# A hybrid decoder step on one Trainium2 core: the last block of gate2 rows is made with the other conditioning blocks, and the first expert weights are looked up later

## The chip, the cores and the metric

One core of one Trainium2 chip runs the whole program. The metric is device microseconds of one execution, the median of repeated runs. TensorE (PE) multiplies, VectorE (DVE), ScalarE (ACT) and GpSimd (POOL) do the elementwise work, and SyncE (SP) issues the weight loads. The five engines run their own instruction streams in order and meet at semaphores.

## The reference, cut to what matters

576 tokens (512 of a prompt, 64 of eight samples) go through one layer. Nine conditioning vectors (one for the prompt, one for each sample) give six rows each, of which `gate2` scales the result of the expert layer at the very end.

```python
ada = jax.nn.silu(c) @ prm['w_ada'][l] + prm['b_ada'][l]
sh1, sc1, g1, sh2, sc2, g2 = jnp.split(ada, 6, axis=-1)
xm = x * (1.0 + sc1[:, None, :]) + sh1[:, None, :]
proj = xm @ prm['w_in'][l]
...
merged = (gates[..., 0, :] * (ya @ prm['w_br_a'][l]) + gates[..., 1, :] * (yb @ prm['w_br_b'][l])
          + gates[..., 2, :] * (yc @ prm['w_br_c'][l]) + gates[..., 3, :] * (yd @ prm['w_br_d'][l]))
mix = merged @ prm['w_o'][l]
x = _layer_norm(DN_ALPHA * x + g1[:, None, :] * mix, prm['ln1_g'][l], prm['ln1_b'][l])
xm2 = x * (1.0 + sc2[:, None, :]) + sh2[:, None, :]
f = _hier_moe(xm2, prm['router_g'][l], prm['router_e'][l], prm['w_e_gate'][l], prm['w_e_up'][l],
              prm['w_e_down'][l])
x = _layer_norm(DN_ALPHA * x + g2[:, None, :] * f, prm['ln2_g'][l], prm['ln2_b'][l])
```

The expert layer picks two of 32 SwiGLU experts for each token; each expert has gate and up matrices of 1024x512 and a down matrix of 512x1024.

## The kernel before, in words

**Stages.** In order of time: shift1 and scale1 (until about 33 us); the branches' projections, their own work and their gated products with `w_br`, branch by branch in the order C, B, A, D (until about 761 us); the product with `w_o`, the first LayerNorm and the router's logits for five token tiles in the order `ORD = (0, 1, 4, 2, 3)` (until about 843 us); the router's decisions (`route`), the first two places (`start_moe`); the experts, two at a time, as 16 pairs (`moe`, about 859 to 1352 us); a loop for tokens that found no place (`overflow`, empty here), and the second LayerNorm (`final`).

**Weights.** Every weight tile of 512 KB is loaded on SP's queue by `Pipe.fill` (L242) in the order of one list, `plan`. For each tile `where` names the buffers it takes. In the projections these are four of the tag `raw`; loaded tiles are split into a high and a low part by ACT (L316) and DVE or POOL (L322), unless they are of the kinds `wa`, `w1`, `w2` or belong to the experts. Expert tiles rotate over 26 buffers: 8 of `raw` and `rb`, 10 of `m8`, 8 of `hi` and `lo`. Expert loads keep the program's order among themselves on SP; tile 27 waits until the two tiles of the first matmul pair are read.

**The conditioning blocks.** Shift2, scale2, gate1 and gate2 are eight blocks of 512 columns, each made of four tiles of `w_ada`. Blocks 0 to `NL` - 1 are made during branch A's gates (`gates("A", ...)`, d = 0 to 7): `ada_block` (L577) multiplies two of the four tiles before the branch product of d and `ada_late` two behind it, as four 32-row matmuls side by side in the array, then ACT and DVE add the four parts (L643 to L647) and POOL adds the rows to the DRAM tile `adad` (L648). With `NL` = 7, block 7 (the second half of gate2) is left: its four tiles, called `w2`, stand in the plan behind the first `GA` = 4 expert tiles, and `ada_gate2` (L663) multiplies them as 9-row matmuls that are put behind the last transposes and router logits of the last two token tiles. The last `m` of the eight is read by ACT (L665) and added to `adad` by POOL (L666). The buffers of the four `w2` tiles then serve the last four of the first 26 expert tiles.

**The router and the first places.** Router logits (L1508, L1510) of the last token tile end the LayerNorm stage. `route` (DVE, L1554 to L1573) makes the choice `Mb`, small matmuls (L1578, L1579) count places, `place` finds the tokens of a pair of experts (L1640, L1651), and `fetch` (L1667 to L1670) gathers their rows by an indirect DMA on POOL. Behind the second of the index casts (L1668) DVE has in its stream: the residual rows (L1516, L1517), then, mixed, the routing weights (`weights`, to `Whl`, L1603 and L1604) and the table of blocks (`blocks`, to `nbi`, L1631).

**The first pair of experts.** `gate_up` multiplies eight gate tiles, then eight up tiles (L1746), in four steps of two tiles each (c = 0 to 3); behind c = 1 and c = 3 it calls `some(n, m)`, which issues n combine pieces and m `parts`. All of these matmuls keep the program's order on PE. Before, one part is issued in each of the four slots of pair 0: `weigh(0)` (L1651, needs `Whl`) behind c = 1 of the gate, `columns(1)` (transposes of the second pair's rows, L1683) behind c = 3, `weigh(1)` and `place(2)` in the up half. The routing weight that `weigh(0)` makes is first read when the down product of pair 0 is scaled (L1714).

**One register load.** `overflow` reads the number of blocks into a register of every engine (`nb = nc.values_load(s.nbi[0:1, 0:1], ...)`, L1855). On SP this load stands among the expert tiles' loads, at a place that is fixed when the program is built.

Of the kernel before, what the change touches and what calls it, by code (L numbers as in the profile page):

```python
# [20 lines left out]
F32 = mybir.dt.float32  # L21
# [169 lines left out]
BME = lambda nc: nc.vector  # L191
HP0 = 2000
N0 = 8
GA = 4
NL = 7
GM = (1, 1, 1, 1, 1)
ND = 6
NW = 3
BP = 1
# [3 lines left out]
class Pipe:  # L203


    def __init__(s, k, plan, hi_pool, nh, where, bufs):
        s.k, s.plan, s.hip, s.nh, s.where, s.bufs = k, plan, hi_pool, nh, where, bufs
        s.nl = s.ns = s.ng = 0
        s.raw, s.hl, s.held, s.dma, s.rel, s.hook = {}, {}, {}, {}, [], {}

        s.m8free, s.m8n, s.m8cur = 0, 0, None

        s.raws = set(i for i, c in enumerate(plan) if c[0] in ("w1", "w2", "wa") or i >= k.moe0)

    def fill(s):
        nc = s.k.nc
# [61 lines left out]
        return ws[0][0] if n == 1 else [w[0] for w in ws]  # L278

    def get(s, nm):  # L280
        while s.plan[s.ng][0] in ("w1", "w2", "wa"):
            s.ng += 1
        i = s.ng
        assert s.plan[i][0] == nm, (s.plan[i][0], nm)
        s.ng += 1
        s.fill()
        s.split()
        s.fill()
        return s.hl.pop(i)

    def pair(s, nm):

        while s.plan[s.ng][0] == "w2":
            s.ng += 1
        i = s.ng
        assert s.plan[i][0] == s.plan[i + 1][0] == nm, (s.plan[i][0], nm)
        s.ng += 2
        s.fill()
        ws = [s.raw.pop(j) for j in (i, i + 1)]
        for _, tag, rc in ws:  # L300
            if rc is not None:
                rc[0] -= 1
            if rc is None or rc[0] == 0:
                s.rel.append(tag)
        return [w[0] for w in ws]


class K:
# [198 lines left out]
    def plan_front(s):  # L507
        A = s.A
        pl = []
        for i in range(16):  # L510
            pl.append(("w1", A["wa1"][i], 1024))
        for i in range(12):
            pl.append(("ct", A["wct"][i], 1024))

        def gates(k, w, kt):
            pl.append(("gl", A["wgl"][k * 8], 1024))
            for d in range(8):
                if d < 7:
                    pl.append(("gl", A["wgl"][k * 8 + d + 1], 1024))
                late = k == 0 and d < NL  # L520
                if late:
                    for h in range(AB):
                        pl.append(("wa", A["wa"][d, h], 1024))
                pl.append(("br", w[d], kt * 128))
                if late:
                    for h in range(AB, 4):
                        pl.append(("wa", A["wa"][d, h], 1024))
        gates(2, A["wbr"][16:24], 4)
        for i in range(12, 16):
            pl.append(("ct", A["wct"][i], 1024))  # L530
        for i in range(4):
            pl.append(("wv", A["wv"][i], 1048))
        gates(1, A["wbr"][8:16], 4)
        for i in range(16, 30):
            pl.append(("ct", A["wct"][i], 1024))
        gates(0, A["wbr"], 4)
        for i in range(30, 36):
            pl.append(("ct", A["wct"][i], 1024))
        gates(3, A["wbd"], 6)

        s.wo0 = len(pl)
        for _ in range(2):
            for k in range(8):
                pl.append(("wo", A["wo"][k], 1024))
        s.moe0 = len(pl)
        s.mi = {}

        def add(nm, ap):
            if len(s.mi) == GA:
                s.wag = len(pl)  # L550
                for i in range(NL * 4, 32):
                    pl.append(("w2", A["wa"][i // 4, i % 4], 1024))
            s.mi[len(pl)] = len(s.mi)
            pl.append((nm, ap, 1024))

        def pair(e, c0, c1):
            for c in range(c0, c1):
                for i in range(2):
                    add(("wg", "wu", "wd")[c // 4], A["we"][e + i, c])
        pair(0, 0, 8)  # L560
        for e in range(0, 32, 2):
            if e < 30:
                pair(e + 2, 0, 8)
            pair(e, 8, 12)
        s.plan = pl
        s.nwa = 0
# [70 lines left out]
    def ada_late(s, b, p):  # L637
# [8 lines left out]
            nc.scalar.copy(r, p[g:g + 9])  # L646
            nc.vector.tensor_tensor(o, o, r, OP.add)  # L647
        nc.gpsimd.dma_start(s.adad[:, b * 512:b * 512 + 512], o, accum_op=OP.add)  # L648

    def ada_gate2(s):  # L650

        nc = s.nc
        a = [s.trs[ORD[4], 0], s.trs[ORD[4], 1], s.lgs[ORD[4]], s.trs[ORD[3], 0], s.trs[ORD[3], 1], s.lgs[ORD[3]]]
        q = [x for x, m in zip(a, GM) for _ in range(m)]
        for b in range(NL, 8):
            p = s.ms()
            for h in range(4):
                w = s.pipe.take(s.wag + 4 * (b - NL) + h)
                for kk in range(2):
                    k = 2 * h + kk  # L660
                    x = q.pop(0) if q else a[-1]
                    with s.tc.issue_after(x.ins), s.tc.high_priority(offset=300):
                        nc.tensor.matmul(p[:9], s.sil[:, k, :9], w[:, kk * 512:(kk + 1) * 512], start=(k == 0), stop=(k == 7))  # L663
            o = s.lp.tile([9, 512], F32, name="g2", tag="xt", bufs=2)
            nc.scalar.copy(o, p[:9])  # L665
            nc.gpsimd.dma_start(s.adad[:, b * 512:b * 512 + 512], o, accum_op=OP.add)  # L666

    def cond_rows(s):

# [603 lines left out]
    def build2(s):  # L1273
# [72 lines left out]
        for i in range(base, len(s.plan)):  # L1346
            m = s.mi.get(i, -1)
            if m < 0 or len(seq) < GA:
                t = (s.ring, "raw") if n9 % (NR + NB) < NR else (s.raw2, "rb")
                n9 += 1  # L1350
                if seq and m < 0:
                    late.append(t)
            elif len(seq) < GA + len(late):
                t = late[len(seq) - GA]
            else:
                t = seq[-(GA + len(late))]
            tags[i] = t
            if m >= 0:
                seq.append(t)
# [54 lines left out]
        rp = s.g2p  # L1414
        s.LG = rp.tile([128, 5, 36], F32, name="LG")
        nc.vector.memset(s.LG, 0.0)
        s.trs, s.lgs = {}, {}
        acc = {}

        def wo(t, k, w):  # L1420
# [48 lines left out]
    def ln1(s, t, acc):  # L1469
# [30 lines left out]
        for h in range(2):  # L1500
            p = s.ms() if P is None else P[:, h]
            for k in range(4):
                kk = 4 * h + k
                s.trs[t, h] = nc.tensor.transpose(p[:, k * n:(k + 1) * n], src[:, kk * 128:(kk + 1) * 128], s.cc("ident")[:n, :n])
            nc.scalar.copy(xt[:, 4 * h:4 * h + 4, :n], p[:, :4 * n].rearrange("p (k t) -> p k t", k=4))
        p = s.ms()
        for k in range(8):
            s.lgs[t] = nc.tensor.matmul(p[:n, :36], xt[:, k, :n], rt[:, k, :], start=(k == 0), stop=(k == 7))  # L1508
        if t < 4:
            V.scalar_tensor_tensor(s.LG[:, t, :], p[:, :36], rstd, s.rb, op0=OP.mult, op1=OP.add)  # L1510
        else:
# [252 lines left out]
    def moe(s):  # L1764
# [42 lines left out]
            n = iter(slots)  # L1807
            return s.gate_up(lambda k, o: s.xg[p][:, k, o * 64:o * 64 + 64], lambda c: c % 2 and some(*next(n)))
        s.columns(0)
        parts += [(lambda: s.weigh(0, s.ms()),), (s.columns, 1), (lambda: s.weigh(1, s.ms()),), (s.place, 2)]  # L1810
        h = s.hidden(gu(0, [(0, 1)] * 4), pe=s.pe)
        for p in range(16):
            if 0 < p < 14:
                parts.append((s.place, p + 2))
# [167 lines left out]
def body(tc, A, NB=4):  # L1982
    with ExitStack() as ctx:
# [1 line left out]
        k.NB = NB  # L1985
        k.build()
        k.build2()
        k.ada_gate2()
        k.route(0, 5, k.lp)
        k.start_moe()  # L1990
        k.le.close()
# [28 lines left out]
```

## Time and profile before

| | |
|---|---|
| median of 3 runs | 1388.23 us (1386.42 to 1388.26) |
| the profiled execution | 1388.56 us |
| its span, first to last instruction | 1386.7 us |
| PE busy | 1309.0 us, 94% of the span |
| DVE, ACT, POOL busy | 776.7, 408.8, 320.4 us |
| HBM | 307.16 MB read, 9.78 MB written, 229 GB/s over the span |
| mean granted TensorE clock | 0.953 |

The span is what the first and last instruction bound; 1.9 us of the profiled time lie around it. A matmul record's end is modelled, so PE's busy time says that something was in the engine, not that it worked at its peak; an fp32 matmul leaves two records. Idle time in square brackets is that of the engine just before the row, with what ended it.

### The profile page before, as it was taken

To read this page: it belongs to the slowest core of one execution; us is meant where nothing else is said; L and a number is where in the kernel's file an instruction comes from. 1 tells how busy PE (TensorE), PEld (TensorE's weight loads), DVE (VectorE), ACT (ScalarE), POOL (GpSimd) and SP (SyncE) were. 2 spreads that over 40 slices of the span, in tenths; PEclk is the share of its full clock that TensorE was granted. 3 is DMA by queue.
4 is the path that set the end of the run, shared out by engine and by line. 5 is a ranking of instruction groups with operands and counts; after the bars stand their busy time and mean duration, and the time that the engine had idled before them with its cause. 6 is when DMAs were issued, how large, how long until landed. Compare 5 with 4: busy or idle time off the path is not lost. (4 is left out here: it accounts for less than half of the span.)

```text
span 1386.7 us, 20311 instructions
## 1 busy us (share of the span) xinstructions
PE 1309.0 (94%) x7962; PEld 944.1 (68%) x7962; DVE 776.7 (56%) x1333; ACT 408.8 (29%) x657; POOL 320.4 (23%) x335
## 2 busy tenths in 40 slices
PE   7997899999999999999999987999999999999992
PEld 5997899999999877788899863344334444444331
DVE  3799797572676356667524487244444334434347
ACT  3311222642463424556422332021111111111114
POOL 1796004051321315333333151000000000000003
PEclk6998999999999989899999997999999999999997
DMA  9522123222322354361222969899999999999972
GB/s 378 151 76 61 54 92 110 69 69 84 108 77 84 113 200 170 129 230 43 72 85 93 320 241 358 340 414 414 414 415 414 415 413 415 414 415 415 415 296 99
DMA packets 90376, 318.15 MB, mean 229 GB/s; under 512 B 11113, under 2 KB 11265, under 8 KB 90271
## 3 DMA queue, kind: packets, MB, share of 16 engines
q1 hardware_dynamic: 83176, 293.29, 55.6%
q0 software_dynamic: 6528, 22.63, 4.8%
q8 instruction: 63, 1.03, 0.3%
q10 hardware_dynamic: 576, 0.93, 0.2%
q14 instruction: 33, 0.27, 0.1%
HBM read 307.16 MB, written 9.78 MB: 229 GB/s over the span
## 5 line engine op out<-in xcount | busy, mean ns | idle before, releaser
L1746 PE MATMUL mh<-raw,xg 128*64 128x512 f32 x1024 | 247.7, 605 | 0.2 <-DMA raw<-in_we_dram 0.2
L589 PE MATMUL mm<-xh,wh 128*128 128x288 f32 x1088 | 244.0, 305 | 2.9 <-DVE ebs L708 2.4
L589 PE MATMUL mm<-xh,wl 128*128 128x288 f32 x1088 | 240.4, 302 | 2.1 <-DVE wl L322 2.1
L589 PE MATMUL mm<-xl,wh 128*128 128x288 f32 x1088 | 240.4, 301 | 0.0
L316 ACT CAST wh<-raw 128x1024 fp32r<-128x1024 f32 (+3 forms) x120 | 113.1, 948 | 316.5 <-PE mm L589 228.3
L322 DVE TENSOR_TENSOR wl<-raw,wh 128x1024 fp32r<-128x1024 f32 (+3 forms) x112 | 133.3, 1194 | 130.1 <-ACT wh L316 129.7
L589 PEld LDWEIGHTS mm<-xh,wh 128*128 128x128 f32 x1088 | 180.9, 194 | 5.7 <-issue 3.3
L589 PEld LDWEIGHTS mm<-xh,wl 128*128 128x128 f32 x1088 | 178.8, 192 | 4.8 <-DVE wl L322 3.2
L589 PEld LDWEIGHTS mm<-xl,wh 128*128 128x128 f32 x1088 | 179.2, 193 | 0.4 <-issue 0.3
L1746 PEld LDWEIGHTS mh<-raw,xg 128*64 128x64 f32 x1024 | 75.2, 138 | 132.8 <-issue 117.4
L1793 DVE TENSOR_TENSOR x<-x,mc 128x512 f32<-128x512 f32 x120 | 78.2, 682 | 124.3 <-PE mc L1732 124.3
L1703 PE MATMUL mh<-raw,h 128*64 128x512 f32 x512 | 130.2, 601 | 1.0 <-ACT h L1761 0.7
L1670 POOL DMA_INDIRECT gr<-xmd,idi x16 | 16.2, 1010 | 415.9 <-PE mh L1746 385.4
L720 DVE SCALAR_TENSOR_TENSOR acc<-ebp,prm,acc 128x512 f32<-128x512 f32 x120 | 104.9, 883 | 2.1
L1703 PEld LDWEIGHTS mh<-raw,h 128*64 128x64 f32 x512 | 40.4, 136 | 72.0 <-issue 56.6
L1715 ACT CAST yh<-y 128x512 fp32r<-128x512 f32 x32 | 19.8, 620 | 220.9 <-DVE y L1714 207.4
L632 POOL TENSOR_TENSOR merged<-merged,sg 128x576 f32<-128x576 f32 x23 | 43.2, 1877 | 108.9 <-DVE sg L631 108.8
L1714 DVE SCALAR_TENSOR_TENSOR y<-mh,ws,G 128x512 f32<-128x512 f32 x32 | 24.0, 751 | 70.2 <-PE mh L1703 70.2
L1732 PEld LDWEIGHTS mc<-yh,ohT 128*128 128x128 f32 x120 | 22.4, 187 | 52.1 <-issue 47.1
L1732 PE MATMUL mc<-yh,ohT 128*128 128x512 f32 x120 | 53.6, 447 | 0.0
L1750 ACT ACTIVATE sg<-mh 128x512 f32<-128x512 f32 x16 | 9.6, 597 | 128.5 <-issue 78.6
L1732 PE MATMUL mc<-yl,ohT 128*128 128x512 f32 x120 | 47.4, 395 | 0.0
(436 smaller groups left out, 2010.3 us busy)
## 6 DMA issues: line engine op xcount, KB each, us to landing
raw<-in_we_dram SPq DMA_DIRECT2D x384, 512.0 KB
raw<-in_wa_dram SPq DMA_DIRECT2D x48, 512.0 KB
raw<-in_wct_dram SPq DMA_DIRECT2D x36, 512.0 KB
raw<-in_wgl_dram SPq DMA_DIRECT2D x32, 512.0 KB
raw<-in_wo_dram SPq DMA_DIRECT2D x16, 512.0 KB
raw<-in_wbr_dram SPq DMA_DIRECT2D x24, 256.0 KB
s<-in_st_ssm_dram POOLq DMA_DIRECT2D x4, 768.0 KB, 4.8
out_ssms_dram<-s POOLq DMA_DIRECT2D x4, 768.0 KB, 4.7
```

The costliest lines, as they stand in the source:

```text
L316: r = s.nc.scalar.copy(out, in_)
L322: r = (s.nc.gpsimd if pool else s.nc.vector).tensor_tensor(out, full, hi, OP.subtract)
L589: nc.tensor.matmul(p[:m, hf, :288], w, xk[:, hf * 288:(hf + 1) * 288], start=(k == 0 and n == 0), stop=(k == kt - 1 and n == 2))
L632: (nc.vector if nm == "D" and d == 7 else nc.gpsimd).tensor_tensor(m, m, sg, OP.add)
L720: nc.vector.scalar_tensor_tensor(o, i, wt, o, op0=OP.mult, op1=OP.add)
L1670: s.glast = nc.gpsimd.indirect_dma_start(out=gr[:n], out_offset=None, in_=s.xmd[:, :], in_offset=bass.IndirectOffsetOnAxis(ap=ix[:n, 0:1], ...
L1703: s.dlast = s.pe(nc.tensor.matmul(p[r], h[:, f, r], ws[o][:, kk * 512:(kk + 1) * 512], start=(f == 0), stop=(f == 3), skip_group_check=True))
L1714: V.scalar_tensor_tensor(y, p, ws, s.G2[0][:, hf * 512:hf * 512 + 512], op0=OP.mult, op1=OP.mult)
L1715: nc.scalar.copy(yh, y)
L1732: m = pe(s.nc.tensor.matmul(p[:r], oT[:n, t * 128:t * 128 + r], y[:n, hf], start=(i == 0), stop=(i == 1)))
L1746: s.pe(nc.tensor.matmul(p[o * 64:o * 64 + 64], xg(k, o), ws[o][:, kk * 512:(kk + 1) * 512], start=(k == 0), stop=(k == 7), skip_group_chec ...
L1793: nc.vector.tensor_tensor(o, o, p[:n], OP.add)
```

## The change

The four tiles of conditioning block 7 are loaded and multiplied in branch A's gates at d = 7, as blocks 0 to 6 are (`NL` = 8); `ada_gate2`, its nine-row matmuls, its copy and its addition to `adad` are gone. `GA` is 8: the first eight expert tiles take the eight buffers of `raw` and `rb`, where before four expert tiles and four `w2` tiles took them; the number of buffers of expert tiles stays 26. In the first pair of experts no part is issued behind c = 1 of the gate; `columns(1)` comes behind c = 3 as before, `weigh(0)` behind c = 1 of the up half, and `weigh(1)` and `place(2)` both behind its c = 3.

```diff
-GA = 4
-NL = 7
-GM = (1, 1, 1, 1, 1)
+GA = 8
+NL = 8
...
         def add(nm, ap):
-            if len(s.mi) == GA:
-                s.wag = len(pl)
-                for i in range(NL * 4, 32):
-                    pl.append(("w2", A["wa"][i // 4, i % 4], 1024))
             s.mi[len(pl)] = len(s.mi)
...
-    def ada_gate2(s):
-
-        nc = s.nc
-        a = [s.trs[ORD[4], 0], s.trs[ORD[4], 1], s.lgs[ORD[4]], s.trs[ORD[3], 0], s.trs[ORD[3], 1], s.lgs[ORD[3]]]
-        q = [x for x, m in zip(a, GM) for _ in range(m)]
-        for b in range(NL, 8):
-            p = s.ms()
-            for h in range(4):
-                w = s.pipe.take(s.wag + 4 * (b - NL) + h)
-                for kk in range(2):
-                    k = 2 * h + kk
-                    x = q.pop(0) if q else a[-1]
-                    with s.tc.issue_after(x.ins), s.tc.high_priority(offset=300):
-                        nc.tensor.matmul(p[:9], s.sil[:, k, :9], w[:, kk * 512:(kk + 1) * 512], start=(k == 0), stop=(k == 7))
-            o = s.lp.tile([9, 512], F32, name="g2", tag="xt", bufs=2)
-            nc.scalar.copy(o, p[:9])
-            nc.gpsimd.dma_start(s.adad[:, b * 512:b * 512 + 512], o, accum_op=OP.add)
...
             if m < 0 or len(seq) < GA:
                 t = (s.ring, "raw") if n9 % (NR + NB) < NR else (s.raw2, "rb")
                 n9 += 1
-                if seq and m < 0:
-                    late.append(t)
...
-        parts += [(lambda: s.weigh(0, s.ms()),), (s.columns, 1), (lambda: s.weigh(1, s.ms()),), (s.place, 2)]
-        h = s.hidden(gu(0, [(0, 1)] * 4), pe=s.pe)
+        parts += [(s.columns, 1), (lambda: s.weigh(0, s.ms()),), (lambda: s.weigh(1, s.ms()),), (s.place, 2)]
+        h = s.hidden(gu(0, [(0, 0), (0, 1), (0, 1), (0, 2)]), pe=s.pe)
...
         k.build2()
-        k.ada_gate2()
         k.route(0, 5, k.lp)
```

## Rows read from the trace of the kernel before

**Rows 1.** Page, 40 equal slices of the span: what the DMA engines moved
```profile
GB/s 378 151 76 61 54 92 110 69 69 84 108 77 84 113 200 170 129 230 43 72 85 93 320 241 358 340 414 414 414 415 414 415 413 415 414 415 415 415 296 99
```

**Rows 2.** Stretches: busy us (records) by engine, clock, DMA share, GB/s
```profile
850.00:860.00 10.00, 4.64 (x25) 3.88 (x27) 8.96 (x16) 1.76 (x5) 4.93 (x6) 0.56 0.95 327
860.00:870.00 10.00, 6.19 (x25) 2.34 (x23) 9.82 (x42) 1.44 (x2) 0.00 (x0) 0.84 0.50 177
870.00:880.00 10.00, 10.00 (x49) 3.85 (x47) 1.65 (x4) 1.65 (x3) 0.00 (x0) 0.91 0.79 288
...
900.00:950.00 50.00, 50.00 (x234) 20.07 (x230) 20.80 (x38) 10.06 (x18) 1.90 (x2) 1.00 1.03 415
...
1335.00:1345.00 10.00, 9.32 (x40) 3.85 (x39) 6.18 (x10) 2.90 (x5) 0.00 (x0) 1.00 0.75 302
```

**Rows 3.** Waits of SP, 890 to 1350 us: us in total, times, longest
```profile
SPq L242 <- DMA raw<-in_we_dram: 310.1, 332, 2.2
```

**Rows 4.** Timeline of SP: the expert tiles' issues around the stall
```profile
848.56 0.33 SPq L242 DMA_DIRECT2D raw<-in_we_dram  x1
862.42 0.80 SPq L242 DMA_DIRECT2D raw<-in_we_dram  x2
870.64 0.81 SPq L242 DMA_DIRECT2D raw<-in_we_dram  x2
```

**Rows 5.** Waits of SP 863.5 to 872 us, and the register load L1855 on SP
```profile
SPq L1855 <- DVE ws L1660: 6.7, 1, 6.7
...
L1855 SPq TENSOR_LOAD <-nbi x1: 472/472/472, 869.7 to 869.7; - x1
```

**Rows 6.** Timeline, DVE: second index cast, `Whl`, `nbi`
```profile
852.76 0.15 DVE L1668 CAST idi<-idf 128x1 int32<-128x1 f32 x1
...
867.50 0.38 DVE L1604 TENSOR_TENSOR Whl<-W,Whl 128x128 fp32r<-128x128 f32 x2
...
869.56 0.14 DVE L1631 CAST nbi<-ca 1x1 int32<-1x1 f32 x1
```

**Rows 7.** Timeline, PE, first pair of experts
```profile
857.60 1.94 PE L1683 MATMUL ms<-cst,gr 128*128 128x128 f32 x8 [4.78 <-DMA gr<-xmd,idi]
859.47 4.64 PE L1746 MATMUL mh<-raw,xg 128*64 128x512 f32 x16
867.92 0.83 PE L1651 MATMUL ms<-Whl,oh 128*128 128x6 f32 x5 [3.81 <-DVE Whl L1604]
...
874.79 3.65 PE L1746 MATMUL mh<-raw,xg 128*64 128x512 f32 x16
```

**Rows 8.** Timeline, the end of the router's logits and the choice
```profile
835.37 1.83 PEld L1508 LDWEIGHTS ms<-rg,xt 128*128 128x128 f32 x8
...
838.28 0.58 ACT L1505 COPY xt<-mm 128x512 f32<-128x512 f32 x1 [1.68 <-PE mm L1504]
...
838.45 3.15 PE L663 MATMUL ms<-raw,sil 128*9 128x512 f32 x4
...
841.53 1.75 PE L1508 MATMUL ms<-rg,xt 128*128 128x36 f32 x14
...
843.21 5.32 PE L663 MATMUL ms<-raw,sil 128*9 128x512 f32 x12
...
847.43 0.33 DVE L1573 TENSOR_TENSOR Mb<-m,m 128x160 bf16<-128x160 f32 x1
848.45 0.10 PEld L1579 LDWEIGHTS <-tsb 128*128 128x128 bf16 x1 [0.86 <-issue]
```

**Rows 9.** Timeline, conditioning block 6 in branch A's gates
```profile
594.54 1.07 PE L577 MATMUL ms<-raw,sil 128*32 128x512 f32 x8
...
598.38 1.06 PE L577 MATMUL ms<-raw,sil 128*32 128x512 f32 x8
```

**Rows 10.** Stretches in branch A's gates, columns as in rows 2
```profile
570.00:575.00 5.00, 3.18 (x26) 2.06 (x24) 3.33 (x13) 2.50 (x5) 0.85 (x2) 0.98 0.00 2
575.00:580.00 5.00, 4.90 (x37) 1.98 (x36) 3.28 (x8) 1.15 (x3) 4.13 (x4) 0.68 0.38 136
```

More of the change, by code (lines that the diff above doesn't have):

```diff
@@ L211, in __init__ @@
         s.m8free, s.m8n, s.m8cur = 0, 0, None
-        s.raws = set(i for i, c in enumerate(plan) if c[0] in ("w1", "w2", "wa") or i >= k.moe0)
+        s.raws = set(i for i, c in enumerate(plan) if c[0] in ("w1", "wa") or i >= k.moe0)
     def fill(s):
@@ L280, in get @@
     def get(s, nm):
-        while s.plan[s.ng][0] in ("w1", "w2", "wa"):
+        while s.plan[s.ng][0] in ("w1", "wa"):
             s.ng += 1
@@ L291, in pair @@
     def pair(s, nm):
-        while s.plan[s.ng][0] == "w2":
-            s.ng += 1
         i = s.ng
@@ L1416, in build2 @@
         nc.vector.memset(s.LG, 0.0)
-        s.trs, s.lgs = {}, {}
         acc = {}
@@ L1503, in ln1 @@
                 kk = 4 * h + k
-                s.trs[t, h] = nc.tensor.transpose(p[:, k * n:(k + 1) * n], src[:, kk * 128:(kk + 1) * 128], s.cc("ident")[:n, :n])
+                nc.tensor.transpose(p[:, k * n:(k + 1) * n], src[:, kk * 128:(kk + 1) * 128], s.cc("ident")[:n, :n])
             nc.scalar.copy(xt[:, 4 * h:4 * h + 4, :n], p[:, :4 * n].rearrange("p (k t) -> p k t", k=4))
@@ L1507, in ln1 @@
         for k in range(8):
-            s.lgs[t] = nc.tensor.matmul(p[:n, :36], xt[:, k, :n], rt[:, k, :], start=(k == 0), stop=(k == 7))
+            nc.tensor.matmul(p[:n, :36], xt[:, k, :n], rt[:, k, :], start=(k == 0), stop=(k == 7))
         if t < 4:
```

## The prediction

> **What bounds the kernel now.** I read the slices of the page first. In the first half the DMA engines move mostly 50 to 230 GB/s; from the middle of the expert stage on they move 414 GB/s in slice after slice [rows 1]. The table of stretches says the same: in 900 to 950 us the DMA share is at its highest value, 1.03, at 415 GB/s, and it falls only behind 1335 us [rows 2]. The waits of SP agree: of the time between 890 and 1350 us SP spends 310.1 us, in 332 waits, on earlier expert tiles' own transfers [rows 3], not on a buffer. So the 384 expert tiles (384 x 0.524 MB = 201 MB, 486 us at 414 GB/s) set the length of that stage, and its end moves only with the moment from which the stream flows without a break. One tile costs 0.524 MB / 414 GB/s = 1.27 us. Ahead of it, in the projections, PE is the bound.
>
> The break is the next thing to see. Twenty-six tiles are on their way by 848.56 us, all buffers are taken, and the next issues come at 862.42 (two tiles) and then only at 870.64 us [rows 4]. Between 860 and 870 us DMA is half idle, and 870 to 880 us still moves 288 GB/s [rows 2]. The first part of the pause ends with PE: its first matmul pair starts at 859.47 us [rows 7]. The second doesn't. The first 16 records (c = 0 and c = 1) are over at 859.47 + 4.64 = 864.1 us [rows 7], so the buffers of the next two tiles are free then, six microseconds before they are loaded. The waits of SP name what holds it: the register load L1855, 6.7 us, and the load itself starts at 869.7 us [rows 5], just behind `nbi`, which DVE ends at 869.56 + 0.14 = 869.70 us [rows 6]. SP works in order, so the tile loads behind L1855 wait for a number that the empty overflow loop needs 480 us later. This hidden wait decides what the change can bring.
>
> **The change, part by part.**
>
> *Block 7 in branch A's gates.* A block costs PE two groups of eight records, 1.07 and 1.06 us [rows 9], 2.1 us, where PE is the bound: +2.1 us for all that follows. Its ACT and DVE adds and its four loads run beside PE there, on a DMA system that is half idle; I cost them at nothing. If that cover fails, it is rival three.
>
> *`ada_gate2` and its nine-row matmuls.* Of its 16 records four (3.15 us) stand in front of the last 14 records of the router's logits, which PE does from 841.53 to 843.28 us; their input was copied at 838.28 + 0.58 = 838.86 us [rows 8]. Without the four, the 14 follow from about 838.5 us. The clock is at half there; eight loads of this kind took 1.83 us [rows 8], 0.23 each, so 14 take 3.2 us and end at 841.7 us: 1.6 us earlier (2.7 us if they ran at the 1.75 us they had). The other twelve records hold PE until 848.45 us, while DVE had `Mb` ready at 847.43 + 0.33 = 847.76 us [rows 8]; of these 0.69 us I take 0.5, since a handoff costs something. Against this, PE is then idle between 841.7 and about 846 us and its clock falls to 1.2 GHz before the counting and place matmuls: some 18 small records on the path, each at most 0.23 - 0.125 us (1.75 / 14) slower, 1.9 us at most, nothing at least. The granted clock was down to 0.56 in 850 to 860 us anyway [rows 2], so a part was slow before; I take 0.4. The chain to the index casts gains 1.6 + 0.5 - 0.4 = 1.7 us (bounds 0 and 3.4).
>
> The Trainium skill ("TensorE: Matmul & The Clock Gate", section "HAM oscillation — how this bites in real kernels") says that pauses of PE put its clock back to half and the next burst starts slow; it speaks against taking filler matmuls away. The rows agree that it happens here.
>
> *Four loads less ahead of the experts.* They took 4 x 1.27 = 5.1 us of DMA. All 26 buffers still fill before PE reads the first; the pause only begins earlier. Nothing, as long as the stream pauses anyway. If the pause were gone, it could be worth up to 5.1 us. The gather, for which PE waited 4.78 us [rows 7], meets less traffic; that too lies in the pause.
>
> *`weigh(0)` later.* It takes 3.81 us of idle PE out of the first gate product: PE waited for `Whl` (867.88 us) [rows 6, 7]. In the new order eight gate tiles, `columns(1)` and four up tiles stand in front, 3 x 3.65 us of matmuls and more [rows 7], so `weigh(0)` comes when `Whl` is long there. But PE isn't the bound of the stage. What it does is free buffers sooner: by the time SP is released, ten or more are free instead of four, and the stream starts at full rate. Before, 870 to 880 us lost (415 - 288) x 10 / 415 = 3.1 us of transfer, 0.64 of it ahead of the issue at 870.64; the remaining 2.4 us are the first transfer's way and a shortage of free buffers. No row parts them: a gain between 0 and 2.4 us; I take a third, 0.8.
>
> *The moment of release.* From the second index cast (852.76 us) to `nbi` (869.56 us) DVE is busy (8.96 and 9.82 of 10 us) [rows 2, 6] with work that the change doesn't touch. So `nbi` moves with the casts, 1.7 us earlier, and SP with it.
>
> The sum: + 2.1 - 1.7 - 0.8 = -0.4 us. The profiled execution took 1388.56 us, 0.33 above the median of 1388.23; from the median this gives 1387.8 us. Its own range, by the bounds (chain 0 to 3.4, restart 0 to 2.4, handing 2.1 in front), is 1384.5 to 1390.3 us.
>
> **The rivals.**
>
> *One: the register load falls behind more tiles.* Its place on SP, between tiles 28 and 29, is fixed when the program is built, and the change moves both sides of it: PE no longer stops behind c = 1, and the gather meets less traffic. Each pair of tiles that gets ahead of it flows in the pause and is worth 2 x 1.27 = 2.5 us. One pair: 1385.3 us. Three or more, or none held at all: the stream runs from the first release, 862.42 - 1.7 = 860.7 us; before, it was worth an unbroken start at 870.64 + 0.8 - 2.5 = 868.9 us; 8.2 less 2.1 is 6.1 us, 1382.1 us. For it: c = 1 was over six microseconds before SP was let go, so the order is out of step with the run. Against: nothing in the change touches L1855 or `nbi`.
>
> *Two: it falls ahead of tiles 27 and 28.* Then the change doesn't bring even the earlier restart: 1387.8 + 2.5 = 1390.3 us. Nothing speaks for it but that the order is made anew.
>
> *Three: the front stalls (slower).* In branch A's gates four buffers serve gate, conditioning and branch tiles in one line. At d = 7 there is no further gate product, and branch tile 7 and the next projection's tiles now stand behind four more loads. If PE waits for one, it loses the wait and then the clock: 570 to 575 us has 1.8 us of idle PE, and 575 to 580 us ran at 0.68 [rows 10], 1.6 us more. Such a gap or two on top of the sum gives some 4 us, 1391.8 us. It decides when PE idles over 3 us there. Against: blocks 0 to 6 go through the same line, and state matmuls of branch D can fill.
>
> *Four: the cold clock eats the chain's gain.* With 1.9 instead of 0.4 us and a logits gain at its low end, `nbi` isn't earlier: 1387.8 + 1.7 = 1389.5 us. By the Trainium skill's rule above this would be the time.
>
> **How the numbers follow.** Forecast 0.34; rival one with one pair 0.22, with three or more 0.22; two 0.05; three 0.10; four 0.07. The single likeliest is the forecast, 1387.8 us. The range that leaves 2 in 10 out reaches to the full rival one and to three: 1381.5 to 1391.5 us. A measurement tells 0.2%, 2.8 us, from no change: below 1385.4 lie all of the large rival one, a good half of the small one and the forecast's edge, 0.40; above 1391.0 lie most of three and edges of the others, 0.15; 0.45 between.
>
> **What would show it.** Right: two issues, L1855 with a wait of some 7 us, then issues in a row; `nbi` as far behind the second index cast as before (16.9 us); PE without the 3.8 us gap; L577 with 128 records; the experts' last load about 0.5 us earlier than at present, while branch D's first matmuls are 2 us later. Wrong: four or more tiles between the pause and L1855, or SP without a wait there (faster); an idle PE and a low clock near 600 us (slower); a DVE stream in which `nbi` has another place.

## The result, and the profile after

The changed kernel takes 1398.0 us (median), the kernel before 1388.7 in the same comparison: ratio 1.0059, 95% interval 1.0046 to 1.0072. It became slower, by 8.2 us as the ratio counts it (the medians lie over 9 us apart); 1387.8 had been forecast, in a range up to 1391.5. The profiled execution took 1398.33 us, with a span of 1396.3.

Line numbers shift a little in the kernel after: the conditioning blocks' matmuls are L570, the projections' L582, tile loads L241, the expert matmuls L1718, the register load L1827. First the expert start, of which the forecast's gains were to come. Its timeline in the kernel after, DVE:

```profile
862.86 0.15 DVE L1640 CAST idi<-idf 128x1 int32<-128x1 f32 x1
```

PE:

```profile
867.53 1.94 PE L1655 MATMUL ms<-cst,gr 128*128 128x128 f32 x8 [4.61 <-DMA gr<-xmd,idi]
869.40 8.81 PE L1718 MATMUL mh<-raw,xg 128*64 128x512 f32 x32
...
882.75 0.72 PE L1623 MATMUL ms<-Whl,oh 128*128 128x6 f32 x5
```

SP's waits between 863.5 and 890 us (total, times, longest), and the register load's own row:

```profile
SPq L1827 <- DVE nbi L1603: 5.3, 1, 5.3
...
L1827 SPq TENSOR_LOAD <-nbi x1: 477/477/477, 879.2 to 879.2; - x1
```

The second index cast starts at 862.86 us, 10.1 later than in [rows 6], and the register load at 879.2, 9.5 later than in [rows 5]. The 3.81 us of idle PE in [rows 7] are gone: 32 records run through, and the places come at 882.75. SP still stops on `nbi`, for 5.3 us. But the first w_o matmul had already come 11.8 us later (773.1 against 761.2 us). So everything behind w_o's start gained (the last down matmul is at 1357.5 against 1348.6, 8.9 later), and the loss lies ahead of it.

The stretches around the end of branch A show it. Kernel before, columns as in rows 2:

```profile
595.00:670.00 75.00, 75.00 (x579) 66.78 (x572) 54.69 (x114) 44.73 (x61) 26.53 (x26) 1.00 0.35 121
670.00:700.00 30.00, 26.67 (x186) 26.23 (x186) 12.67 (x9) 13.00 (x16) 11.52 (x7) 0.94 0.19 63
```

Kernel after:

```profile
595.00:670.00 75.00, 70.70 (x490) 59.66 (x490) 53.15 (x112) 37.44 (x55) 27.59 (x27) 0.89 0.40 136
670.00:700.00 30.00, 28.62 (x211) 27.82 (x210) 14.14 (x12) 16.53 (x20) 5.92 (x5) 1.00 0.24 76
```

Length less busy time times granted clock is the PE time that a stretch lost. Before: nothing from 595 to 670 us, and 30 - 26.67 x 0.94 = 4.9 behind it. After: 75 - 70.70 x 0.89 = 12.1, and 1.4 behind. That is 8.6 us more; with block 7's own matmuls, up to 2.1 us, it makes 10.7. The stretch from the sigmoid of branch A's last gate to that of branch D's last grew by 10.3 us (156.7 to 167.0).

What PE did there, in the kernel after's timeline:

```profile
599.90 1.06 PE L570 MATMUL ms<-raw,sil 128*32 128x512 f32 x8
...
603.18 1.79 PE L1197 MATMUL ms<-cx,s 128*64 128x8 f32 x16 [1.59 <-DMA s<-in_st_ssm_dram]
...
609.86 1.22 PE L582 MATMUL mm<-yA,wh 128*128 128x288 f32 x4
...
616.67 1.93 PE L570 MATMUL ms<-raw,sil 128*32 128x512 f32 x16
...
624.25 0.85 PE L582 MATMUL mm<-xh,wh 128*128 128x288 f32 x2 [2.21 <-ACT wh L313]
```

SP's issues of tiles, in the same timeline:

```profile
597.15 0.81 SPq L241 DMA_DIRECT2D raw<-in_wa_dram  x2
600.99 0.33 SPq L241 DMA_DIRECT2D raw<-in_wbr_dram  x1
601.41 5.67 SPq L241 DMA_DIRECT2D raw<-in_wa_dram  x2
617.76 12.80 SPq L241 DMA_DIRECT2D raw<-in_wct_dram  x6
```

SP's longest wait between 607 and 618 us:

```profile
SPq L241 <- PE ms L570: 10.7, 1, 10.7
```

Stretches of 5 us, columns as in rows 2:

```profile
605.00:610.00 5.00, 5.00 (x39) 4.72 (x40) 3.14 (x8) 0.93 (x2) 0.85 (x1) 0.50 0.41 141
...
620.00:625.00 5.00, 2.50 (x14) 1.69 (x11) 3.68 (x11) 2.40 (x4) 0.38 (x1) 0.87 0.97 353
625.00:630.00 5.00, 5.00 (x21) 4.24 (x20) 5.00 (x9) 3.83 (x8) 3.48 (x3) 0.50 0.57 207
```

Block 7's first two tiles were issued at 597.15 us, where (at 596.06) the kernel before issued the next projection's first tile. Their matmuls are not run in two halves around a product, as block 6's were [rows 9], but all sixteen together at 616.67 us, behind branch product 7 and behind state work (branch D's state-space steps, many small ones on PE, ACT, DVE and POOL, whose result goes into that branch's norm). Until then the tiles hold the line of four buffers; SP waits 10.7 us for those matmuls, and the next projection's first tile is issued at 617.76. PE runs dry (2.5 of 5 us in 620 to 625) and is granted 0.50 of its clock, 1.2 GHz, in 625 to 630, as it was in 605 to 610 behind the 1.59 us of idle time at 603. The rule of the Trainium skill that the prediction cited ("TensorE: Matmul & The Clock Gate", section "HAM oscillation — how this bites in real kernels": pauses of PE bring the clock down to half) agrees with these rows.

The clock fell where the fillers had been, too. Stretches from just before the last copy of the router's input, columns as in rows 2, in the kernel before:

```profile
838.00:843.00 5.00, 5.00 (x22) 2.24 (x20) 2.25 (x2) 0.58 (x1) 0.54 (x1) 0.70 1.02 414
843.00:848.00 5.00, 5.00 (x15) 1.17 (x14) 4.07 (x27) 0.00 (x0) 0.00 (x0) 1.00 1.03 419
848.00:853.00 5.00, 3.47 (x32) 2.63 (x30) 2.66 (x11) 1.86 (x2) 1.90 (x2) 0.83 1.03 415
```

The same 12 us later in the kernel after:

```profile
850.00:855.00 5.00, 3.53 (x18) 3.38 (x16) 2.24 (x9) 1.87 (x2) 0.53 (x1) 0.50 1.03 419
855.00:860.00 5.00, 0.94 (x15) 0.76 (x15) 3.76 (x24) 0.00 (x0) 0.00 (x0) 0.50 1.03 419
860.00:865.00 5.00, 2.59 (x15) 2.44 (x15) 3.62 (x10) 0.32 (x2) 2.46 (x2) 0.50 0.60 189
```

So PE was granted 0.50 there all the way, instead of 0.70 to 1.00. It cost little: the chain to the index casts still became shorter (its figures stand below, in the account of the prediction).

### The profile page after: what moved, and what is told of

The parts are those of the page before. It is cut to its first block, busy times and chain, and to the rows that moved or that the text cites. A ratio compares the mean times of both kernels' runs of the same rounds, so it can differ in the third digit from the quotient of the medians.

```text
span 1396.3 us, 20309 instructions
## 1 busy us (share of the span) xinstructions
PE 1318.2 (94%) x7962; PEld 954.6 (68%) x7962; DVE 779.9 (56%) x1336; ACT 407.0 (29%) x656; POOL 318.7 (23%) x335
## 3 DMA queue, kind: packets, MB, share of 16 engines
q8 instruction: 63, 1.03, 0.3%
## 5 line engine op out<-in xcount | busy, mean ns | idle before, releaser
L582 PE MATMUL mm<-xh,wh 128*128 128x288 f32 x1088 | 243.2, 304 | 7.1 <-ACT wh L313 3.5
L1718 PE MATMUL mh<-raw,xg 128*64 128x512 f32 x1024 | 249.2, 603 | 0.4 <-DMA raw<-in_we_dram 0.3
L582 PE MATMUL mm<-xh,wl 128*128 128x288 f32 x1088 | 240.3, 301 | 2.2 <-DVE wl L319 2.2
L582 PE MATMUL mm<-xl,wh 128*128 128x288 f32 x1088 | 240.2, 302 | 0.0
L582 PEld LDWEIGHTS mm<-xh,wh 128*128 128x128 f32 x1088 | 180.4, 194 | 10.4 <-ACT wh L313 4.2
L582 PEld LDWEIGHTS mm<-xh,wl 128*128 128x128 f32 x1088 | 179.2, 193 | 4.4 <-DVE wl L319 3.3
L582 PEld LDWEIGHTS mm<-xl,wh 128*128 128x128 f32 x1088 | 179.5, 194 | 0.7 <-issue 0.7
L1718 PEld LDWEIGHTS mh<-raw,xg 128*64 128x64 f32 x1024 | 75.7, 137 | 134.9 <-issue 117.4
L624 DVE TENSOR_TENSOR sg<-mm,sg 128x576 f32<-128x576 f32 x24 | 18.2, 757 | 57.7 <-PE mm L582 57.6
```

What stands on the lines that cost most here:

```text
L582: nc.tensor.matmul(p[:m, hf, :288], w, xk[:, hf * 288:(hf + 1) * 288], start=(k == 0 and n == 0), stop=(k == kt - 1 and n == 2))
L624: a = nc.vector.tensor_tensor(sg, q[:, :, :288], sg, OP.mult)
L1718: s.pe(nc.tensor.matmul(p[o * 64:o * 64 + 64], xg(k, o), ws[o][:, kk * 512:(kk + 1) * 512], start=(k == 0), stop=(k == 7), skip_group_chec ...
```

## The experiments

The expectations of e1 to e4 speak of three theories: one, block 7's four tiles hold up the line of four buffers and starve PE at the end of branch A; two, the loss comes from the fillers and the later lookup at the expert start; three, block 7's matmuls, adds and bank are in the way at that place, not its tiles. Those from f1 on name theirs in words.

The front's own pace varies by several us from execution to execution: the sigmoid of branch A's last gate came at 596.0 us in the kernel before and at 592.3 in g4, whose front is the same. So the front is compared by the stretch from that sigmoid to that of branch D's last gate, in profiled executions, with 156.7 us before; "stretch +10.3" means 10.3 us more. Each is one execution, but kernels with the same front agree closely: 156.6 to 156.7 us in the kernel before, e2 and g4, 167.0 to 167.2 in the kernel after, e1 and h3. Ratios are to the kernel before, run beside it, with 95% intervals. They are coarser: the kernel before itself took 1388.7 to 1390.1 us beside the kernel after and e1 to g4, but 1392.0 beside h1 to h3, so these three ratios may stand too low.

**Which of the two changes? e1 and e2**

e1 is the kernel after with the old slots:
```diff
-        parts += [(s.columns, 1), (lambda: s.weigh(0, s.ms()),), (lambda: s.weigh(1, s.ms()),), (s.place, 2)]
-        h = s.hidden(gu(0, [(0, 0), (0, 1), (0, 1), (0, 2)]), pe=s.pe)
+        parts += [(lambda: s.weigh(0, s.ms()),), (s.columns, 1), (lambda: s.weigh(1, s.ms()),), (s.place, 2)]
+        h = s.hidden(gu(0, [(0, 1)] * 4), pe=s.pe)
```


> The kernel after with the four slots of the first pair of experts as before, so the change of block 7 alone. Theory one (the line of four buffers at the end of branch A starves PE): all of the loss is in it; the w_o product starts 10 to 12 us later than before, and the run is 8 to 11 us slower than before, about 1 us slower than the kernel after. Theory two (the lost filler matmuls and the later lookup cost time at the start of the experts): with the old slots half or more of the 9 us come back, 1390 to 1394 us.

Ratio 1.0058 (1.0037 to 1.0078), stretch +10.6: block 7 carries the whole loss.

e2 is the kernel before with the new slots, the same lines the other way round.

> The kernel before with the new slots of the first pair alone. Theory one: block 7 isn't touched, so no loss; the stream of expert tiles restarts without a shortage of buffers, 0 to 2.4 us faster than before, 0.8 by the prediction's term. Theory two: slower than before by 2 us or more.

Ratio 0.9993 (0.9974 to 1.0013), stretch 0.0, and 478.3 us from `nbi` to the last down matmul against 479.0. The later lookup neither costs nor gains anything that can be told.

**Tiles, adds or PE? e3, f2 and f3**

e3, no tiles for block 7:
```diff
-                late = k == 0 and d < NL
+                late = k == 0 and d < 7
...
+        if b == 7:
+            ws = [s.cst[:, 0:512]] * 2
...
```


> The kernel after, but block 7 is multiplied with a constant that lies in SBUF already, so its four tiles are not loaded and take no buffer (its values are left out; its 16 matmul records, adds and the rest stay at their place). Theory one: the loads are the cause, so the idle PE and the low clock around 620 us go and the w_o product starts 2 to 4 us later than before instead of 11.8; the run comes to 1386 to 1391 us. Theory three (the matmuls, adds and PSUM of block 7 at that place are the cause, not the loads): still 6 us or more slower than before.

Ratio 1.0032 (1.0009 to 1.0056), stretch +8.1. The time lies between the two expectations; the w_o product starts at 771.5 us, as theory three has it. The gaps at 600 to 630 us were gone (74.12 us busy at 1.00 in 595 to 670), yet 670 to 700 us now lost 30 - 21.75 x 0.89 = 10.6 us. A row of PE's timeline in e3:

```profile
685.93 2.29 PE L730 MATMUL mm<-xs,cst 128*128 128x288 f32 x4 [8.25 <-POOL xs L1276]
```

PE waits 8.25 us in front of branch D's norm, since the state work that feeds it ends later. In the kernel before the same row has 3.33 us:

```profile
675.97 1.24 PE L752 MATMUL mm<-xs,cst 128*128 128x288 f32 x4 [3.33 <-POOL xs L1298]
```

Theory one, the line of buffers alone, falls here: it explains where the kernel after lost its time, but with the tiles gone another path is nearly as late.

f2, no tiles (by the edit of e3) and no adds or store:
```diff
...
         p = s.ada_block(b, range(AB, 4), p)
+        if b == 7:
+            return
```


> The kernel after, with block 7's eight matmuls on constant columns, its tiles not loaded, and its adds and its store left out (that block's values are left out). What is left of the moved block is 2.1 us on PE. If the adds, the store and what queues behind them were the loss that stayed without the tiles, the w_o start is 762.5 to 764.5 and the time 1385 to 1388 (2 us above the kernel before at the w_o start, 2.9 us less behind it). If the order of PE's work or the bank of the sums alone is enough, the w_o start stays at 769 to 772 and the time at 1393 to 1395.

Ratio 0.9968 (0.9949 to 0.9988), stretch +1.3. The block's matmuls alone cost 1.3 us, and what the kernel gains behind them is then seen in the total.

f3, tiles loaded and held, 8 of 512 columns multiplied, no adds or store (by the edit of f2):
```diff
+            n = 8 if b == 7 else 512
+            s.nc.tensor.matmul(p[32 * i:32 * i + 32, :n], s.sil[:, 2 * hs[0] + i], ws[i // 2][:, i % 2 * 512:i % 2 * 512 + n],
...
```


> The kernel after, with block 7's four tiles loaded and held as in it, but only 8 of their 512 columns multiplied, and its adds and its store left out (that block's values are left out). The theory of the line of four buffers: PE still runs out of projection tiles at the end of branch A, w_o start 768 to 771, time 1391 to 1395. The theory that the adds and the store are the loss and the tiles are not: w_o start 761 to 763, time 1384 to 1388. If each of the two alone makes most of the loss (two ways side by side, the later one counts), this run shows 768 to 771 and the run without adds and tiles 763.

Ratio 1.0011 (0.9993 to 1.0030), stretch +6.5. The line of buffers is a loss by itself. So: matmuls 1.3, held tiles 6.5, adds and store 8.1 - 1.3 = 6.8, all three 10.3. The last two run side by side: they would add up to more than the 10.3, and curing one of them bares the other. In the kernel after PE hardly waits for the input of branch D's norm, being late itself by then (it had lost 12.1 us by 670 us):

```profile
688.07 1.24 PE L727 MATMUL mm<-xs,cst 128*128 128x288 f32 x4 [0.41 <-POOL xs L1273]
```

**Why do the adds cost that much? f1, g1, g2 and h1** (all without block 7's tiles)

f1, the conditioning rows read back behind block 6:
```diff
-        s.cond_rows()
...
                 s.ada_late(d, pa)
+                if d == 6:
+                    s.cond_rows()
```


> The kernel after, with block 7 multiplied with constant columns and its four tiles not loaded (that block's values are left out), and the conditioning rows read back from device memory behind block 6 instead of behind block 7. The theory that the four tiles in the line of buffers are the whole loss has nothing more to give here: as without the tiles alone, the w_o start about 771 (before: 761.2), the time 1393 to 1395. The theory that block 7's store and the six transfers behind it stand ahead of branch D's state work on the POOL queue: the state work ends 5 to 8 us sooner than without the tiles alone, w_o start at 763 to 766, time 1386 to 1389. The theory that it is the adds on ACT and DVE and the bank they hold, not the POOL queue: w_o start still 769 or later.

Ratio 1.0066 (1.0047 to 1.0085), stretch +10.6: no gain, so the place of those transfers alone isn't it.

g1, the PSUM bank freed by one copy, the same adds behind it:
```diff
+        if b == 7:
...
+            nc.scalar.copy(r, p)
+            nc.scalar.copy(o, r[32:41])
+            nc.vector.tensor_tensor(o, r[0:9], o, OP.add)
...
```


> The kernel after without block 7's tiles (constant columns, that block's values left out), as before, but its four partial sums are copied to SBUF whole by one ACT instruction, and the same two DVE and ACT steps of each strip then run on the copy: one ACT instruction more, the same adds, the same store; the PSUM bank is free behind the first copy. Theory of the bank (one of four, held from 621.9 to 632.5 us while branch D's state work asks for banks): w_o start 760 to 764, time 1386 to 1388.5, the idle PE before branch D's norm 3 to 4 us as before instead of 8.3. Theory of the engines' time (six ACT and DVE steps, 3.8 us, stand between the state work's own): w_o start 769 to 772, time 1393 to 1396.

Ratio 1.0032 (1.0010 to 1.0055), stretch +8.9: the bank isn't it either.

g2, one strip of nine rows, one copy:
```diff
...
+                s.nc.tensor.matmul(p[:9], s.sil[:, 2 * hs[0] + i, :9], ws[0],
+                                   start=(hs[0] == 0 and i == 0), stop=(hs[0] > 0 and i == 3))
...
+        if b == 7:
+            nc.scalar.copy(o, p[0:9])
...
```


> The same kernel without block 7's tiles (values left out), but its eight matmuls add up in one strip of nine rows, so that one ACT copy and the store are all that is left of the adds. Both theories expect the w_o start at 760 to 764 and 1386 to 1388.5 us; the theory that the store on the POOL queue and the conditioning reads behind it do the harm expects 767 to 772 and 1392 to 1395.

Ratio 1.0003 (0.9983 to 1.0023), stretch +3.3. The expectation overlooked PE: in this form the sixteen records take 7.0 us instead of 1.9 (a row of its timeline):

```profile
613.66 7.04 PE L574 MATMUL ms<-cst,sil 128*9 128x512 f32 x16
```

PE's wait for the norm fell to 1.1 us. The last step of the state work ends 84.3 us behind branch A's last sigmoid here, 87.7 in e3 and 81.1 in f2. So with the five further ACT and DVE steps 8.1 - 3.3 = 4.8 us of the adds' 6.8 went, although PE's form is longer; the other 2.0 are the copy, the store and PE's longer form, which no run parts.

h1, the adds run twice:
```diff
+        if b == 7:
+            for g in (32, 64, 96):
+                nc.scalar.copy(r, p[g:g + 9])
+                nc.vector.tensor_tensor(o, o, r, OP.add)
```


> The kernel after without block 7's tiles (constant columns, that block's values left out), with six more ACT and DVE steps on its sums: three more copies of a strip and three more adds, behind the first ones; the matmuls and the store as without the tiles alone. Measured from the sigmoid of branch A's last gate to that of branch D's last, in profiled executions: before 156.7 us, without tiles and adds 1.3 more, with one copy in place of the adds 3.3 more, with the adds 8.1 more. Theory: the loss that stays without the tiles is the steps' own place in the queues of ACT and DVE, between the steps of branch D's state work; then doubling the adds costs 3 to 7 us more, 11 to 15 more than before, and the time is 1396 to 1401. Rival: the built order flips once when there is anything at all behind block 7, and the number of steps does not matter: 8 to 10 more than before, 1393 to 1395.

Ratio 1.0033 (1.0006 to 1.0059), stretch +10.4: 2.3 us for six more steps, less than the theory's 3 to 7 and more than the rival's nothing. Each is half right: the first six steps cost 6.8 us with the store, six further ones a third of that.

What the first ones set off stands in the traces. Timeline of e3, POOL:

```profile
632.91 0.80 POOL L644 DMA_DIRECT2D adad<-ao  x1 [3.78 <-DVE S L1209]
633.64 1.33 POOL L655 DMA_DIRECT2D cr<-adad  x2
...
635.98 1.59 POOL L1115 TENSOR_TENSOR D<-aT,cst 24x768 fp32r<-24x768 f32 x1
637.41 0.94 POOL L1103 TENSOR_TENSOR xdd<-xd,dst 128x384 f32<-128x384 f32 x1
638.20 1.53 POOL L1276 TENSOR_TENSOR xs<-xs 128x576 f32<-128x576 f32 x1
639.58 1.10 POOL L1143 TENSOR_TENSOR cx<-ea,bc 128x384 f32<-128x384 f32 x1
```

And DVE:

```profile
630.80 0.55 DVE L1138 TENSOR_TENSOR E<-E,cbm 128x384 f32<-128x384 f32 x1
...
636.78 4.34 DVE L1138 TENSOR_TENSOR E<-E,cbm 128x384 f32<-128x384 f32 x1
```

POOL stands 3.78 us in front of block 7's store, whose last add DVE starts at 631.94 us; then it issues the transfers, and four arithmetic steps, most of which had gathered behind them, run in one row, 635.98 to 640.68 us. A DVE step of the state work with two SBUF operands, 0.55 us at most places, lasts through that row: 4.34 us. In h1 the same kind of step took 5.13 us (beside POOL's issues of transfers and two arithmetic steps), in g1 a step of 0.35 us took 4.00 (DVE's timeline of g1):

```profile
636.72 4.00 DVE L1221 TENSOR_TENSOR S<-S,ea 128x192 f32<-128x192 f32 x1 [1.24 <-PE ms L1205]
640.82 0.35 DVE L1222 TENSOR_TENSOR S<-S,ms 128x192 f32<-128x192 f32 x1
```

That is 3.7 to 4.6 us too long in one step of the state work. How much of it reaches the norm is not shown. Counted from branch A's last sigmoid, e3 is 1.6 us behind f2 where this step starts and 5.4 where it ends, but 2.6 at the last step of this kind and 6.6 at the norm. Some of the lag comes at the very end: from the state's last step (L1213 in e3) to the norm e3, g1, h1 and f1 take 12.5 to 13.5 us, the kernel before and f2 11.4, and in those four ACT runs a gate's sigmoid between the last steps of the state work. In the kernel after itself no such step took over 1.6 us, so the long step belongs to what the kernels without the tiles lose, not to how the kernel after lost its 10.3 us.

The Trainium skill ("SBUF — State Buffer", section "SBUF: two separate sides") says that VectorE and GpSimd share a pair of ports as an exclusive lock, held for a whole instruction, and that a DVE step with two SBUF operands needs it; the rows agree, except that DVE waited for a row of POOL's instructions and not for one. In f1, where no such step was stretched, the state work lost as much in another way, by a later start (its first exponential on ACT behind branch A's last gate comes at 628.3 us, against 620.4 in the kernel before, though branch A's last gate came 3.3 us earlier). That rest hangs on the built order, and no run here parts it further.

**Another place. e4 and h2**

e4, block 7 in branch D's gates, third product, with the new slots:
```diff
-                late = k == 0 and d < NL
+                b = d if k == 0 and d < 7 else 7 if k == 3 and d == DB else None
+                late = b is not None
...
```


> The kernel after, but block 7 is loaded and multiplied in branch D's gates at d = 2, where gate products go on behind it. Theory one: the line there has PE work in front of it, so the block costs its 2.1 us and the rest of the change gives back 2.5: 1386 to 1391 us. Theory three: the block costs as much there, 6 us or more slower than before.

Ratio 0.9979 (0.9960 to 0.9997), stretch +1.2: tiles and adds cost nothing there that can be told. The adds come behind 710 us, when the state work is over (it ends at 674), and SP issues one tile every 4 to 7 us.

h2, beside block 3 at branch A's fourth product:
```diff
-                late = k == 0 and d < NL
+                bs = () if k or d == 7 else (d, 7) if d == A7 else (d,)
...
```


> The kernel after with block 7 multiplied beside block 3 at branch A's fourth product, not beside the last product. Theory of the end of branch A (its last product is where the next projection's tiles and branch D's state work start, and both wait on what block 7 adds there): at the fourth product neither is near, so that only PE's 2 us and a short lack of tiles are lost: the stretch from branch A's last gate to branch D's last is as before (0 to 1 us more), the loss ahead of it 2 to 5 us, time 1387 to 1391. Rival: four more tiles in the line of four buffers starve PE at any product of branch A: 8 us or more ahead of the last gate, 1394 to 1398.

Ratio 1.0017 (0.9994 to 1.0040). Part of the loss lies ahead of branch A's last gate here, so the stretch is taken from the sigmoid of its third gate: 6.4 us more than before, against 13.1 in the kernel after (two executions of one and the same front differ by up to 1.7 in this longer stretch). That is just above the first expectation (2 to 6 us in all) and below the rival's 8: the block costs in the middle of branch A too, but the end is the worse place.

**SP's register load. f4, g4 and h3**

All three issue the register load behind the last expert tile:
```diff
-        nb = nc.values_load(s.nbi[0:1, 0:1], min_val=0, max_val=64)
+        with tc.issue_after(s.pipe.dma[len(s.plan) - 1].ins):
+            nb = nc.values_load(s.nbi[0:1, 0:1], min_val=0, max_val=64)
```
f4 on top of e4; g4 on top of e2; h3 on the kernel after.

> Block 7 in branch D's gates (third product of that branch) instead of the last of branch A, the new slots, and the register load on SP behind the last expert tile's issue. With block 7 there the time was 1387.0 against 1389.4 before, and SP stopped for 5 to 7 us: the DMA engines were busy 0.65 and 0.52 of 850 to 860 and 860 to 870 us, 1.03 behind it. If the tiles' arrival sets the expert stage, the 8.3 us that the engines lacked come back in part: 1379 to 1383. If PE sets it (10.00 of 10 us from 860 on at the full clock), nothing comes back: 1386 to 1388.

> The kernel before (block 7 behind the router, as there) with the new slots of the first places and the register load on SP behind the last expert tile's issue. In branch D's variant the same two steps took the last down matmul from 1346.9 to 1342.9. If SP's stop was worth that much there because the tiles' arrival sets the expert stage, it is worth it here too: 1383 to 1387, last down matmul at 1343 to 1346. If block 7's own matmuls still hold the start back, 1388 to 1390.

> The kernel after with nothing changed but the register load on SP, which is issued behind the last expert tile. From the cast of the row counts to the last down matmul it took 478.4 us in the kernel after, 479.0 in that before, and 475.3 and 476.4 with the load moved (block 7 in branch D, and in its old place with the new slots). If SP's stop costs the same whatever the front did: 475 to 476.5 here, and 1394 to 1396 against 1398. If the old order already hides it once the restart has its covers: 478 and 1397 to 1399.

From `nbi` to the last down matmul: f4 475.3 us (e4 478.9), g4 476.4 (e2 478.3), h3 474.7 (after 478.4): 1.9 to 3.7 us come back. Ratios: f4 0.9951 (0.9931 to 0.9970), the fastest version; g4 0.9978 (0.9955 to 1.0001); h3 1.0003 (0.9982 to 1.0023) where the kernel after has 1.0059. That difference of the ratios, 7.8 us, is more than the traces show; its front is still 10.5 us longer than before, and the kernel before was slow beside it (1392.0). The stretches of h3, columns as in rows 2:

```profile
870.00:880.00 10.00, 10.00 (x44) 3.75 (x42) 9.80 (x39) 2.71 (x4) 0.00 (x0) 0.84 0.79 261
880.00:890.00 10.00, 10.00 (x57) 4.43 (x54) 3.98 (x12) 0.71 (x2) 0.00 (x0) 1.00 1.03 418
```

The same of the kernel after:

```profile
870.00:880.00 10.00, 10.00 (x44) 3.47 (x42) 9.79 (x39) 3.00 (x5) 0.00 (x0) 0.85 0.55 184
880.00:890.00 10.00, 10.00 (x55) 4.50 (x53) 3.96 (x12) 0.59 (x1) 0.00 (x0) 1.00 0.90 346
```

(0.79 - 0.55 + 1.03 - 0.90) x 10 / 1.03 = 3.6 us more of the stream: the 3.7 us that came back.

**The whole, with one strip. g3** (the kernel after, block 7 as in g2)

> The kernel after, whole, with block 7 added up in one strip and copied once. The four tiles still stand in the line of four buffers: as with the tiles alone, w_o start 763.5 to 766 and 1390 to 1393 us, 4 to 7 us less than the kernel after. If tiles and adds only hurt each other's place in the order and not by themselves, it stays at 1396 or more.

Ratio 1.0046 (1.0026 to 1.0066), stretch +9.7. Both expectations missed: 1395.6 us, and w_o at 772.4. The tiles alone (6.5, f3) and this form alone (3.3, g2) make 9.8 together, so the likely reason is that the 5.1 us of extra PE eat what the missing adds give back; no run shows it by itself.

## Why the prediction was wrong

**The failing step** is the costing of block 7's cover: "Its ACT and DVE adds and its four loads run beside PE there, on a DMA system that is half idle; I cost them at nothing." The loads took little of the DMA engines (a share of 0.40 instead of 0.35 in 595 to 670 us), but they took all four places of a line that the next projection needs at that moment (6.5 us alone, f3). The adds ran beside PE, but in front of branch D's state work on ACT, DVE and POOL, for which PE waited 3.33 us in front of the norm even before (6.8 us, f2 against e3). A share of busy time showed neither, since both are matters of order.

**Rival three** named the first half of this with its place, its condition and its signs, an idle PE and a low clock near 600 us. It had a chance of 0.10 and a price of 4 us. The argument against it, "blocks 0 to 6 go through the same line", was the mistake: behind those blocks a gate or branch tile follows, for which PE still has a product of work, and their matmuls run in halves around a product; behind block 7 comes the next projection, and the built order ran its matmuls behind everything else. Why the build placed them there was not tried.

**Block 7's matmuls**, +2.1 us: measured 1.3 (f2) and 1.2 (e4).

**The chain to the index casts**, -1.7 us: from the last copy of the router's input to the second index cast 14.5 us in the kernel before, e2 and g4, and 12.6 in the kernel after and all other kernels without `ada_gate2` but f1 (13.6), so -1.9. The size was right; the clock did fall, as the term had it, but from `Mb` to that cast it took 5.2 us against 4.8 to 5.3. `nbi` has moved by more than forecast: 16.0 to 16.4 us behind the cast in the kernels without `ada_gate2`, 16.8 in those with it. Rival four is out.

**The restart**, -0.8 us: 478.4 us instead of 479.0 from `nbi` to the last down matmul, and 478.3 in e2; but the other kernels with the new slots and the register load in its old place have 478.6 to 479.8. Nothing that these runs can tell.

**SP's register load** stayed where it was, with two tiles ahead of it, as forecast; rivals one and two did not come. Its price had been put at up to 8.2 us; moved on purpose it was worth 1.9 to 3.7, since the stream can't run at its full rate until PE has freed buffers (0.79 of 1.03 in 870 to 880 us of h3).

With +10.3 in place of +2.1 in front, the same sum gives 10.3 - 1.7 - 0.8 = +7.8 us; by the ratio it was 8.2 (0.0059 x 1388.7). That it comes so close is partly luck, as the restart's 0.8 was not seen and `nbi`'s further 0.6 not forecast.

## What to carry to other kernels

A load that is small for the DMA engines can be large for the line of buffers that it joins: before work is moved into such a line, count who waits behind it there and when the buffer will be given back in PE's built order. Small steps on ACT, DVE and POOL are free only where none of these engines has to hand something to PE soon; the end of one stage, where the next one's first tiles and its chained work start together, is the worst place, and here the same block cost 1.2 us some 90 us later. When one cause of a stall is taken away and the time hardly moves, look for a second path that was hidden behind it.

## What the runs showed of the hardware

A DVE step with two SBUF operands can be held for a whole row of POOL's instructions: 4.00 (g1), 4.34 (e3) and 5.13 us (h1) for steps that take 0.35 to 0.56 us at their shortest. Not every row does it: beside three POOL steps in a row in f2 (642.46 to 647.56 us) no DVE step took over 1.88 us. Sixteen records of a 512-column matmul took 7.0 us when they summed in one strip of nine rows (g2) and 1.9 us in four strips of 32 (the kernel after), both at a granted clock of 1.00. A register load on SP cost the tile stream 1.9 to 3.7 us (e4, e2 and the kernel after against f4, g4 and h3) by standing in front of loads that didn't need its number.
